# One PSUM tile for two banks, merged adds among the last pairs, and pair 4 loaded in blocks, in a matmul with rotary embedding

## The chip, the core and the metric

The kernel runs on one core of a Trainium2 chip. The metric is the device time of one execution in microseconds. A run executes the kernel under test and the kernel before in turn on the same chip. A ratio is the mean time of one kernel's fast executions over the mean of the other's in the same rounds, so it is not quite the ratio of the medians quoted beside it, which take in all executions. A profile shows one execution, the profiled one.

## The reference

The input is 16 x 512 rows of 768 numbers. All are multiplied by one 768 x 768 matrix, and each 64-wide head of the product is rotated (a "rope").

```python
y = np.matmul(x, weight)                      # x: (16, 512, 768)
y = y.reshape(batch, seq, n_heads, head_dim)  # 12 heads of 64
y1, y2 = y[..., :32], y[..., 32:]
out1 = y1 * cos1 - y2 * sin1                  # cos, sin: (512, 64)
out2 = y2 * cos2 + y1 * sin2
out = np.concatenate([out1, out2], axis=-1)
```

## The kernel before

The 64 units of work have 128 rows each; two units make a pair, so there are 32 pairs (0 to 31). I call the halves of pair 3 "3a" and "3b". A unit is loaded, cast to 16 bits, transposed, multiplied (12 matmuls in the plain case), multiplied by cosine and sine on VectorE (the rope, which reads PSUM) and added up on GpSimd; then the pair is stored.

There are three ways to load and transpose. A **plain pair** comes as two full loads of 384 KB, is cast on ScalarE, transposed on TensorE and copied from PSUM by ScalarE. A **block pair** of the first kind comes as four quarter loads of 192 KB from the SyncE queue; each writes 32 of the 128 partitions in runs of 768 bytes. ScalarE casts it, VectorE transposes it, and TensorE is spared two groups of six transposes. A block pair of the second kind is loaded and cast by GpSimd's DMA queue.

```python
BLOCKS = range(8, 25, 4)              # second kind: 8, 12, ... 24
BLOCKS_SP = (*range(6, 27, 4), 28)    # first kind: 6, 10, ... 26, 28
...
hpool = ...tile_pool(name="hpool", bufs=2)              # block pairs of the first kind
py_pool = ...tile_pool(name="py", bufs=6, space=PSUM)   # six single banks
...
def load_quarter(n, q, eng, dst):     # q-th block of columns -> partitions 32q to 32q+31
    src = x[b : b + 2].rearrange("b (j a r) (q k) -> r q a (b j) k", r=SB, a=R, q=NQ)
    dst = dst.rearrange("p s (j k) -> p (s j) k", j=NQ)
    eng.dma_start(out=dst[ts(q, R)], in_=src[r, q])
...
def psum(n, s):                       # a pair has three banks; each of the last four has 2 x 2
    key, banks = (n, 3) if n < NP - ALONE else ((n, s), 2)
...
for n in range(2, AHEAD - 1):         # pairs 2 to 5, two full loads each
    load_pair(n)
for q in (0, 2, 1, 3):                # then pair 6 in quarters
    load_blocks_sp(AHEAD - 1, q)
...
for n in range(2, NP):
    load_pair(n + AHEAD - 2)
    for q, ahead in ((0, 8), (2, 7), (1, 6), (3, 5)):
        if n + ahead >= AHEAD:
            load_blocks_sp(n + ahead, q)
    ...
    for s in (0, 1):
        i = 2 * n + s
        if n < 4:
            for c0, c1 in ((0, 256), (256, H)):
                for c in CHUNKS:
                    mm(n, s, *c, c0, c1)
                if c0 == 0:
                    upto("turn", i + 2)   # transposes and ScalarE's copies of what is ahead
                    upto("cast", i + 4)   # ScalarE's casts of what is still further ahead
        ...
```

In the views, PE is TensorE, PEld its weight loads, DVE VectorE, ACT ScalarE, POOL GpSimd and SP SyncE; a q marks the issue of an instruction or a transfer. The tile xs holds a plain unit, xf a block pair of the first kind, xh one of the second, xc the cast, xT the transposed unit, psy (and later psw) the product in PSUM, pt a transpose in PSUM, tq the rope, ov the sum.

On ScalarE instructions go in the order of the program (its lines in the views stand in that order: before, the cast of 4a at 21.93 us, then the copy of 3b at 23.52 us). In the loop above, while unit 5 (2b) is multiplied, the cast of unit 8 (4a) is put on ScalarE; the copy of unit 7 (3b) is put there one unit later, so behind that cast. ScalarE also issues the stores of most pairs.

## Time and profile before

| | before |
|---|---|
| median of three executions | 156.14 us |
| span of the profiled execution | 152.3 us |
| TensorE busy | 145.4 us (95%) |
| VectorE, GpSimd busy | 131.2 us, 123.6 us |
| granted TensorE clock | 0.994 |

The span is the time from the first to the last instruction. The decisive view is the chain of work that ended last: TensorE has 92% of it, without a gap. The lines stand in the prediction. The view by windows: after the window (us) come busy times of TensorE, its weight loads, VectorE, ScalarE and GpSimd, then the granted clock, the busy share of the DMA engines and GB/s.

```profile
16.00:22.00 6.00, 6.00 (x56) 4.55 (x55) 6.00 (x6) 4.68 (x7) 4.45 (x6) 1.00 1.04 374
```

### The profile page before, as it was taken

The page shows a single profiled execution, that of the slowest core. Times are in us where ns is not written, and L with a number is a line of the kernel's source. Part 1 is how long each engine was busy: PE and PEld are TensorE (multiplying, and loading weights), DVE is VectorE, ACT ScalarE, POOL GpSimd, SP SyncE. Part 2 cuts the span into 40 slices and gives each one's busy share as a digit, 9 for nine tenths or more (in the row PEclk, how much of TensorE's full clock was granted, in tenths as well). Part 3 has the DMA queues.
Part 4 walks back from the last instruction along what each step waited for, and adds up shares of the span by engine and source line. Part 5 has one row for each costly group of instructions (what it writes and reads, how often), then busy time and mean ns, then how long its engine had stood idle before and what let it go on. Part 6 is the DMA issues. An engine that isn't in the chain of part 4 may idle for free.

```text
span 152.3 us, 2721 instructions
## 1 busy us (share of the span) xinstructions
PE 145.4 (95%) x1038; PEld 92.2 (61%) x1038; DVE 131.2 (86%) x140; ACT 73.6 (48%) x91; POOL 123.6 (81%) x72
## 2 busy tenths in 40 slices
PE   6999999999999999999999999999999999999950
PEld 2556777666656566666656665666666566666620
DVE  0567999779898989989898989989898989997890
ACT  3260696882525726282616624582617547764200
POOL 1000399999998999799997999787888879999990
PEclk9999999999999999999999999999999999999997
DMA  5999999999999999999999999999999999996555
GB/s 134 377 401 400 404 320 244 271 387 340 300 302 405 375 304 356 355 397 291 363 330 347 400 341 239 358 400 402 320 330 404 414 410 401 409 373 235 203 205 195
DMA packets 29037, 51.17 MB, mean 336 GB/s; under 512 B 7264, under 2 KB 15072, under 8 KB 29024
## 3 DMA queue, kind: packets, MB, share of 16 engines
q1 hardware_dynamic: 16640, 29.17, 56.9%
q10 hardware_dynamic: 6944, 19.86, 33.1%
q0 software_dynamic: 5440, 1.97, 10.7%
q8 instruction: 8, 0.13, 0.4%
q14 instruction: 5, 0.04, 0.1%
HBM read 27.79 MB, written 25.17 MB: 348 GB/s over the span
## 4 chain that ended last, share of the span: by engine, by line
PE 92%; DVE 5%; issue 0%; DVEq 0%
PE psy L174 79%; PE pt L140 9%; PE psy L254 4%; DVE tq L188 3%; DVE psy L225 0%; DVE ov L229 0%; DVE xT L78 0%; DVE cold L261 0%; DVE w_sb L126 0%; DVEq L229 0%; DVE tq L225 0%; DVEq L188 0%
## 5 line engine op out<-in xcount | busy, mean ns | idle before, releaser
L174 PE MATMUL psy<-w_sb,xT 128*128 128x256 f16 (+2 forms) x781 | 131.1, 323 | 0.2 <-DVE w_sb L126 0.2
L188 DVE TENSOR_TENSOR tq<-psy,csn 128x1024 f32<-128x1024 f32 (+1 forms) x99 | 111.6, 1167 | 9.6 <-PE psy L174 9.3
L199 POOL TENSOR_TENSOR ov<-tq 128x1536 f32<-128x1536 f32 (+2 forms) x45 | 111.3, 2501 | 8.1 <-DVE tq L188 5.4
L174 PEld LDWEIGHTS <-xT 128*128 128x128 f16 x781 | 74.7, 98 | 44.8 <-ACT xc L76 0.5
L76 ACT COPY xT<-pt 128x768 f16<-128x768 f16 x38 | 30.4, 799 | 57.8 <-PE pt L140 53.5
L76 ACT CAST xc<-xs 128x768 f16<-128x768 f32 x38 | 33.1, 909 | 9.7 <-DMA xs<-in_x_dram 7.7
L140 PEld LDWEIGHTS <-xc 128*128 128x128 f16 x240 | 17.1, 100 | 5.8 <-DVE xc L78 0.9
L140 PE MATMUL pt<-ident,xc 128*128 128x128 f16 x240 | 20.4, 222 | 0.0
L331 POOL COPY mark<-xs 128x1 f32<-128x1 f32 x1 | 0.2, 185 | 15.8 <-DMA xs<-in_x_dram 15.8
L76 ACT CAST xc<-xf 128x768 f16<-128x768 f32 x14 | 12.7, 906 | 0.0
L99 POOL DMA_DIRECT2D xh<-in_x_dram x20 | 11.8, 595 | 0.5 <-issue 0.5
L254 PE MATMUL psy<-cold 128*128 128x512 f16 x17 | 6.9, 557 | 1.2 <-DVE cold L261 1.2
L148 DVE STREAM_TRANSPOSE xT<-xc 128x384 f32<-128x384 f32 x14 | 7.9, 563 | 0.0
L148 DVE STREAM_TRANSPOSE xT<-xh 128x384 f32<-128x384 f32 x10 | 7.0, 700 | 0.0
L126 DVE CAST w_sb<-w_raw 128x768 f16<-128x768 f32 (+2 forms) x7 | 3.4, 500 | 1.7 <-DMA w_raw<-in_weight_dram 1.7
L78 DVE CAST xc<-xs 128x768 f16<-128x768 f32 x2 | 1.9, 948 | 3.2 <-DMA xs<-in_x_dram 3.2
L254 PEld LDWEIGHTS <-cold 128*128 128x128 f16 x17 | 2.0, 131 | 3.5 <-issue 2.2
L78 DVE COPY xT<-pt 128x768 f16<-128x768 f16 x2 | 1.1, 558 | 1.6 <-PE pt L140 1.6
L76 ACT ACT_TABLE_LOAD x1 | 1.3, 1283 | 0.7 <-PEq L408 0.7
L261 DVE MEMSET cold<- 128x256 uint32 x1 | 0.3, 272 | 0.9 <-PEq L408 0.9
L229 DVE TENSOR_TENSOR ov<-psy,tq 128x384 f32<-128x384 f32 x1 | 0.6, 558 | 0.0
L225 DVE TENSOR_TENSOR tq<-psy,csn 128x384 f32<-128x384 f32 x1 | 0.6, 557 | 0.0
(9 smaller groups left out, 1.9 us busy)
## 6 DMA issues: line engine op xcount, KB each, us to landing
out_dram<-ov ACTq DMA_DIRECT2D x25, 768.0 KB, 8.8
xs<-in_x_dram SPq DMA_DIRECT2D x40, 384.0 KB, 9.0
xf<-in_x_dram SPq DMA_DIRECT2D x28, 192.0 KB, 10.3
out_dram<-ov SPq DMA_DIRECT2D x7, 384.0 KB, 2.4
out_dram<-ov SPq DMA_DIRECT2D x3, 768.0 KB, 7.0
w_raw<-in_weight_dram SPq DMA_DIRECT2D x5, 384.0 KB, 6.7
xh<-in_x_dram POOLq DMA_DIRECT2D x20, 96.0 KB, 10.1
w_raw<-in_weight_dram SPq DMA_DIRECT2D x1, 256.0 KB, 5.4
```

The costliest lines, as they stand in the source:

```text
L76: eng.copy(out=o, in_=i_)
L78: eng.tensor_copy(out=o, in_=i_)
L99: eng.dma_start(out=dst[ts(q, R)], in_=src[r, q])
L126: nc.vector.tensor_copy(out=w_sb[:, t, e, c0:c1], in_=w_raw[t, e][:, c0:c1])
L140: nc.tensor.transpose(pt[:, t, e, :], xc[:, t, e, :], ident)
L148: nc.vector.transpose(out=xT.bitcast(FP32).rearrange("p t (j a) o -> p t j (a o)", j=NQ), in_=x16.pop((n, s)).bitcast(FP32).rearrange(orde ...
L174: nc.tensor.matmul(ps[:, a - lo : z - lo], xTT[n, s][:, t, e, :], w_sb[:, t, e, a:z], start=((t, e) == CHUNKS[0] and n > 1), stop=((t, e) ...
L188: nc.vector.tensor_tensor(out=tqs[n][:, :, c0:c1].rearrange("p j (h d) -> p j h d", d=D), in0=ps.rearrange("p (h d) -> p h d", d=D) .unsqu ...
L199: eng.tensor_tensor(out=ovs[n][:, ds(c0, w)].rearrange("p (h t d) -> p h t d", t=2, d=HD), in0=tq[:, 0].rearrange("p (h t d) -> p h t d", ...
L225: nc.vector.tensor_tensor(out=o, in0=ph, op=MULT, in1=csn[:, j, n % SB, :].unsqueeze(1).broadcast_to((P, nh, D)),)
L229: nc.vector.tensor_tensor(out=ovs[n][:, c0:c1].rearrange("p (h t d) -> p h t d", t=2, d=HD), in0=ps.rearrange("p (h t d) -> p h t d", t=2, ...
L254: nc.tensor.matmul(psys[n][b], cold[:, 0:P], cold, start=True, stop=opened[0] < WARM - 6)
```

## The change

It has three intents: two of a pair's three PSUM banks become one wide tile, so that one rope of 2048 elements does the work of two of 1024; the first halves of pairs 28 to 30 get one rope, and all their halves one add; pair 4 becomes a block pair of the first kind, which takes two groups of transposes from TensorE. The third part also changes the order of the first loads, the distances at which quarters are fetched ahead, and the number of buffers for block pairs.

```diff
-    BLOCKS_SP = (*range(6, 27, 4), 28)
+    BLOCKS_SP = (4, *range(6, 27, 4), 28)
...
-    hpool = ctx.enter_context(tc.tile_pool(name="hpool", bufs=2))
+    hpool = ctx.enter_context(tc.tile_pool(name="hpool", bufs=3))
...
-    py_pool = ...(name="py", bufs=6, space=bass.MemoryType.PSUM)
+    py_pool = ...(name="py", bufs=2, space=bass.MemoryType.PSUM)   # 2 single, 2 double
...
+    def bank(wide):
+        return py_pool.tile([P, 1024 if wide else 512], FP32, tag="psw" if wide else "psy", ...)
...
     def rope_bank(n, b):
-        rope(n, b * 512, (b + 1) * 512, psys[n][b])
+        rope(n, 512 * b, 512 * (1 + 2 * b), psys[n][b])
...
-    for n in range(2, AHEAD - 1):
-        load_pair(n)
-    for q in (0, 2, 1, 3):
-        load_blocks_sp(AHEAD - 1, q)
+    load_pair(2)
+    load(3, 0)
+    load_blocks_sp(4, 0)
+    load(3, 1)
+    load_blocks_sp(4, 2)
+    load(5, 0)
+    load_blocks_sp(4, 1)
+    load(5, 1)
+    for m, q in ((4, 3), (6, 0), (6, 2), (6, 1), (6, 3)):
+        load_blocks_sp(m, q)
...
-        for q, ahead in ((0, 8), (2, 7), (1, 6), (3, 5)):
+        for q, ahead in ((0, 7), (2, 6), (1, 6), (3, 5)):
...
+            if not in_halves(n, s):                  # 28a, 29a, 30a
+                for c in CHUNKS:
+                    mm(n, s, *c)
+                rope(n, s * H, (s + 1) * H, psys[n, s][:, 0:H])
+                add(n, s * H, (s + 1) * H, nc.gpsimd)
+                store(n, nc.sync, s * H, (s + 1) * H)
+                continue
...
-                add(n, c0, c1, nc.gpsimd)
+                if n == NP - 1:
+                    add(n, c0, c1, nc.gpsimd)
+                elif hi == H:
+                    add(n, s * H, (s + 1) * H, nc.gpsimd)
```

More of the change, by code (lines that the diff above doesn't have):

```diff
@@ L69 @@
     pt_pool = ctx.enter_context(tc.tile_pool(name="pt", bufs=2, space=bass.MemoryType.PSUM))
-    py_pool = ctx.enter_context(tc.tile_pool(name="py", bufs=6, space=bass.MemoryType.PSUM))
+    py_pool = ctx.enter_context(tc.tile_pool(name="py", bufs=2, space=bass.MemoryType.PSUM))
     w_raw, xss, xhs, x16, xTT, psys, tqs, ovs = {}, {}, {}, {}, {}, {}, {}, {}
@@ L152, in transpose_blocks, with in_halves @@
         xTT[n, s] = xT.rearrange("p t m e -> p t e m")
-    def psum(n, s):
-        key, banks = (n, 3) if n < NP - ALONE else ((n, s), 2)
-        if key not in psys:
-            psys[key] = [
-                py_pool.tile([P, 512], FP32, tag="psy", name="psy") for _ in range(banks)
-            ]
-        ps = psys[key]
-        if banks == 2:
-            return [(ps[k][:, 0:HH], k * HH, (k + 1) * HH) for k in (0, 1)]
-        cut = 512 if s == 0 else 256
-        return [(ps[s][:, ds(s * 256, cut)], 0, cut), (ps[s + 1][:, 0 : H - cut], cut, H)]
+    def bank(wide):
+        return py_pool.tile(
+            [P, 1024 if wide else 512], FP32,
+            tag="psw" if wide else "psy", name="psw" if wide else "psy",
+        )
+    def in_halves(n, s):
+        return s == 1 or n == NP - 1
+    def psum(n, s):
+        if n < NP - ALONE:
+            if n not in psys:
+                psys[n] = bank(False), bank(True)
+            one, two = psys[n]
+            if s == 0:
+                return [(one, 0, 512), (two[:, 0:256], 512, H)]
+            return [(two[:, 256:512], 0, 256), (two[:, 512:1024], 256, H)]
+        if not in_halves(n, s):
+            if (n, s) not in psys:
+                psys[n, s] = bank(True)
+            ps = psys[n, s]
+            return [(ps[:, 0:512], 0, 512), (ps[:, 512:H], 512, H)]
+        if (n, s) not in psys:
+            psys[n, s] = [bank((n, s) == (NP - 1, 1)) for _ in (0, 1)]
+        ps = psys[n, s]
+        return [(ps[k][:, 0:HH], k * HH, (k + 1) * HH) for k in (0, 1)]
     def mm(n, s, t, e, c0=0, c1=H):
@@ L213, in rope_pair @@
     def rope_pair(n):
-        for b in range(3):
+        for b in (0, 1):
             rope_bank(n, b)
@@ L253, in warm @@
             psum(n, 0)
+            ps = psys[n][0] if b == 0 else psys[n][1][:, ts(b - 1, 512)]
             nc.tensor.matmul(
-                psys[n][b], cold[:, 0:P], cold, start=True, stop=opened[0] < WARM - 6
+                ps, cold[:, 0:P], cold, start=True, stop=opened[0] < WARM - 6
             )
@@ L368 @@
             if n < NP - ALONE:
-                for b in ((0,), (1, 2))[s]:
-                    rope_bank(n, b)
+                rope_bank(n, s)
+                continue
+            if not in_halves(n, s):
+                for c in CHUNKS:
[3 more added lines that the diff above has]
+                store(n, nc.sync, s * H, (s + 1) * H)
                 continue
```

## The prediction

> **What bounds the kernel now.** I read the shares of busy time first, then the chain of waits that ended last, then the timelines of the stretches that the diff touches: the first 32 us, where pair 4 is loaded, and the last 25 us, where the last pairs end.
>
> ```profile
> PE 145.4 (95%) x1038; PEld 92.2 (61%) x1038; DVE 131.2 (86%) x140; ACT 73.6 (48%) x91; POOL 123.6 (81%) x72
> ...
> PE 92%; DVE 5%; issue 0%; DVEq 0%
> PE psy L174 79%; PE pt L140 9%; PE psy L254 4%; DVE tq L188 3%; DVE psy L225 0%; DVE ov L229 0%; DVE xT L78 0%; DVE cold L261 0%; DVE w_sb L126 0%; DVEq L229 0%; DVE tq L225 0%; DVEq L188 0%
> ```
>
> TensorE carries 92% of the chain, VectorE only the end. The same chain in order of time shows TensorE without a gap:
>
> ```profile
> 23.15 0.33 PE pt L140 x6
> 23.48 1.97 PE psy L174 x18
> 25.45 0.33 PE pt L140 x6
> 25.79 1.29 PE psy L174 x6
> 27.08 0.34 PE pt L140 x6
> 27.41 1.95 PE psy L174 x12
> ```
>
> One unit (half a pair, 12 matmuls) is 1.95 us, a group of six transposes 0.33 to 0.34 us. So only TensorE's own work, or a new hole in it, moves the time much. VectorE waits 7.9 us for TensorE between 20 and 126 us, and GpSimd 5.4 us for VectorE between 60 and 126 us: both keep up there. At the end all three finish together: TensorE's last matmul at 146.8 us, then three short VectorE operations:
>
> ```profile
> 146.84 0.56 DVE L225 TENSOR_TENSOR tq<-psy,csn 128x384 f32<-128x384 f32 x1
> 147.32 0.56 DVE L225 TENSOR_TENSOR psy<-psy,csn 128x384 f32<-128x384 f32 x1
> 147.91 0.56 DVE L229 TENSOR_TENSOR ov<-psy,tq 128x384 f32<-128x384 f32 x1
> ```
>
> which end at 148.47 us. GpSimd's last adds (130.46 us plus 18.00 us, no gap) end at 148.46 us.
>
> [...] 1024-element ropes go in chains of one in 1.18, two in 2.35, three in 3.45 us; each costs about its elements. [...] ScalarE's casts and copies stand in the order of the program. A cast that waits for data therefore holds the copies behind it. [...]
>
> **The change part by part.** *Pair 4 as a block pair.* Its two groups of TensorE transposes go (2 x 0.335 = 0.67 us off the path) and with them two ScalarE copies of 0.80 us. VectorE gets two stream transposes of 0.56 us, which it can hide. Price: its two loads of 384 KB become four quarter loads of 192 KB in runs of 768 B, and a cast of either half needs all four quarters. Now the order of landing counts. Each load's landing is its issue plus its time to landing: before, pair 3's halves land at 17.0 and 18.0 us, pair 4's at 19.0 and 19.9, pair 5's at 22.7 and 24.4 (13.8 + 8.9, 14.2 + 10.2), pair 6's last quarter at 30.1 (18.0 + 12.1). The step grows from 0.97 us because GpSimd's own small loads then share the engines; the bandwidth falls:
>
> ```profile
> 18.00:20.00 2.00, 2.00 (x24) 1.83 (x22) 2.00 (x3) 1.06 (x2) 2.00 (x4) 1.00 1.06 406
> 20.00:22.00 2.00, 2.00 (x19) 1.45 (x18) 2.00 (x3) 2.00 (x4) 1.99 (x2) 1.00 1.04 317
> 22.00:24.00 2.00, 2.00 (x22) 1.62 (x20) 2.00 (x3) 1.33 (x3) 2.00 (x2) 1.00 1.26 220
> ```
>
> (last columns: granted clock, DMA share, GB/s). In the new order (3a, 4q0, 3b, 4q2, 5a, 4q1, 5b, 4q3, then pair 6) pair 4's last quarter stands behind both loads of pair 5. How long is a quarter? At 400 GB/s 0.49 us; from the stretch 110 to 112 us, where quarters run nearly alone at 231 GB/s, 0.85 us; I choose 0.65 us, as here they alternate with full loads. From 17.0 us: 4q0 17.65, 3b 18.6, 4q2 19.3, 5a 20.2, 4q1 20.9; then contention: 5b 2.2 us, 4q3 1.2 us, so about 24.3 us.
>
> When is it needed? ScalarE's order is cast of 4a, copy of the transposed 3b, cast of 4b:
>
> ```profile
> 21.93 0.92 ACT L76 CAST xc<-xs 128x768 f16<-128x768 f32 x1
> 23.52 0.80 ACT L76 COPY xT<-pt 128x768 f16<-128x768 f16 x1 [0.67 <-PE pt L140]
> ```
>
> The copy of 3b feeds TensorE's matmuls at 24.78 us (23.48 plus 12 matmuls of 0.108). It must start by 23.95, so the cast must start by about 23.1 us (0.82 us from a cast to what follows). With landing at 24.3 us TensorE stands 1.2 us. After it pair 4's transposes on VectorE come in time (cast of 4b would end near 26.7 us, unit 9 starts near 30), and pair 6, later by four quarters less two loads (4 x 0.65 - 1.94 = 0.7 us), finds TensorE later by as much. Net of this part: -0.67 + 1.2 = +0.5 us.
>
> *Second and third bank as one tile.* 28 pairs have two ropes of 1024 elements become one of 2048. From the means 1205 and 953 ns for 1024 and 768 elements the slope is 0.98 ns, so one of 2048 is about 2.21 us against 2.35 for two: 0.14 us each, under 4 us of VectorE in all, beside TensorE: nothing on the path. Both banks now come free together, but pair n + 2 needs them some 4 us after; the rope ends about 2.3 us after its unit, so no wait. TensorE's work is unchanged.
>
> *The last four pairs.* First halves of pairs 28 to 30 get one rope of 1536 elements (estimate 0.953 + 768 x 0.00098 = 1.71 us, against 1.86 for two), all six halves one add instead of two: 6 x (2 x 0.96 - 1.80) = 0.7 us less GpSimd. But the small tiles are only two now: 30's second half takes both and 31's first half follows at once. Call P the end of 30's first half on TensorE. The rope runs from P to P + 1.71; 30b's first quarter-tile can be roped only from about P + 1.63 to P + 2.58, while TensorE wants that bank at P + 0.34 + 1.95 = P + 2.29. It waits about 0.34 us with the signal. Before, with six banks in turn, there is no such wait. GpSimd, followed through the same way, ends its last add near P + 8.16, VectorE near P + 8.23, against P + 7.85 before. So +0.4 us; the saved adds are used up by their later start, as one add waits for both ropes.
>
> Sum: -0.67 + 1.2 + 0.34, that is +0.87 us, on 156.14: **157.0 us**.
>
> **The rivals.** *The quarters arrive in time.* For it: whoever wrote this interleaved the loads with care, and if a quarter costs 0.5 us among full loads the last lands near 23 us and there is no hole. Then -0.67 + 0.34 = -0.3: 155.8 us. Against it: four of them need to overlap, with 220 GB/s at the time. I give it a quarter. *The hole is larger.* At 0.95 us a quarter (the time of the queue's packets, 56.9% of the span, less its other bytes at the stores' rate, shared among 28 quarters) the last lands past 25.5 us, a hole of 2.4 to 4 us: 158.3 to 159.8 us. [...] *VectorE becomes the bound* through two more transposes: it had 7.9 us of waiting, and merging gives more than 1.1 us back, so no. *GpSimd ends last before, and fewer adds help at once*: it ends 0.01 us before VectorE, so at best they save nothing alone.
>
> **Range and chances.** From the first rival with a little noise, 155.5, to a hole of 2.8 us, 158.6. Faster by over 2% needs under 153.0, and nothing on the path offers 3 us: 0.01. Slower by over 2% needs over 159.3, a hole of 3.5 us: 0.06. The rest, 0.93, is within 2%.
>
> **What would show it.** In the changed trace: TensorE transposes 228 instead of 240; ScalarE's cast of pair 4 preceded by a wait for the load near 24 us, then a hole in TensorE's chain near 25 us of 0.5 to 2.5 us, and none if the first rival holds; a wait of about 0.3 us of TensorE for VectorE just before 31's first half; 28 ropes of 1024 elements and 28 of 2048 in place of 84 of 1024, VectorE's busy time down by some 3 us, without effect; last add and last VectorE operation again within 0.2 us. Wrong would make it: quarters that land before 23 us, a stall later in the middle because a prefetch moved, or small banks freed earlier than I work out.

## The result and the profile after

The changed kernel took 164.78 us (median of four, 162.18 to 165.3) against 155.83 us for the kernel before in the same rounds. The ratio of the fast executions is 1.0481, with a 95% interval of 1.0328 to 1.0634. It is slower by nearly 5%, and outside the predicted range. Two of the four executions lie over 1.5% above the fastest and do not count as fast; that leaves two, hence the wide interval.

These are lines of the page of the changed kernel: busy times, then TensorE's busy tenths and granted clock in 40 slices of 4.07 us, then the chain that ended last by engine.

```profile
PE 148.0 (91%) x1026; PEld 91.8 (56%) x1026; DVE 130.4 (80%) x111; ACT 72.0 (44%) x89; POOL 122.7 (75%) x66
...
PE   7999993399999999999999999999899899999870
...
PEclk9999999659999999999999999999999999999999
...
PE 53%; DMA 23%; DVE 11%; POOL 4%; issue 3%; SPq 2%; ACT 1%; ACTq 1%; DVEq 0%
```

Three things are to be seen. TensorE has 12 instructions less (1026 for 1038), as intended, yet more busy time. In the seventh and eighth slice it is three tenths busy, and in the eighth and ninth its clock is at six and five tenths. And transfers, which had no part in the chain before, now have 23% of it. The same chain in order of time shows where it leaves TensorE:

```profile
16.64 12.78 DMA xf<-in_x_dram
...
29.76 0.41 ACTq L260
...
30.31 0.81 ACT xT L76
...
31.16 4.02 PE psw L190 x12
```

The transfer is the last quarter of pair 4. It was issued at 16.64 us and landed 12.8 us later. ScalarE's own order of time shows who waited for it:

```profile
22.51 0.79 ACT L76 COPY xT<-pt 128x768 f16<-128x768 f16 x1
29.52 0.88 ACT L76 CAST xc<-xf 128x768 f16<-128x768 f32 x1 [6.23 <-DMA xf<-in_x_dram]
29.76 0.41 ACTq L260 DMA_DIRECT2D out_dram<-ov  x1
30.31 0.80 ACT L76 COPY xT<-pt 128x768 f16<-128x768 f16 x1
```

ScalarE stood idle for 6.23 us ahead of the cast of 4a; the copy behind that cast is that of 3b, which TensorE needed next. TensorE stood 5.33 us. What follows the hole is in the windows:

```profile
16.00:22.00 6.00, 5.94 (x56) 4.45 (x55) 6.00 (x5) 3.99 (x6) 3.07 (x6) 1.00 1.09 224
...
26.00:30.00 4.00, 0.00 (x0) 0.00 (x0) 1.05 (x1) 0.47 (x1) 4.00 (x2) 0.96 1.33 220
30.00:36.00 6.00, 4.84 (x15) 2.24 (x16) 1.94 (x3) 3.43 (x5) 1.79 (x1) 0.50 1.10 294
```

From 16 to 22 us only 224 GB/s arrive, for 374 before, with the DMA engines no less busy (share 1.09 for 1.04). From 30 to 36 us the clock is 0.50: the two units from 31.16 to 37.84 us took 6.68 us, where two units take 3.90 us at the full clock.

The accounts of the two profiled executions, by when TensorE reaches the same work: the transposes of 5a start at 29.37 us before and at 37.84 us after, 8.47 us later. The hole and a small one ahead of it (0.29 us) make 5.6 us, the low clock 2.8 us, a later start of this execution 0.57 us, and the two transpose groups give back 0.67 us; that sums to 8.3 us. The last transposes start at 140.46 and 150.59 us, 10.13 us later, so the middle loses another 1.7 us. The last VectorE operation ends at 148.47 and 159.25 us, 10.78 us later, so the tail loses some 0.65 us.

### The profile page after: what moved, and what is told of

Read it like the earlier page. It is cut to its first block, busy times and chain, and to the rows that moved or that the text cites.

```text
span 162.8 us, 2672 instructions
## 1 busy us (share of the span) xinstructions
PE 148.0 (91%) x1026; PEld 91.8 (56%) x1026; DVE 130.4 (80%) x111; ACT 72.0 (44%) x89; POOL 122.7 (75%) x66
## 4 chain that ended last, share of the span: by engine, by line
PE 53%; DMA 23%; DVE 11%; POOL 4%; issue 3%; SPq 2%; ACT 1%; ACTq 1%; DVEq 0%
PE psw L190 33%; PE psy L190 16%; DVE tq L204 9%; DMA xf<-in_x_dram 8%; DMA out_dram<-ov 7%; POOL ov L215 4%; DMA xs<-in_x_dram 4%; DMA w_raw<-in_weight_dram 4%; PE pt L140 4%; DVE xT L148 1%; SPq L83 1%; ACT xT L76 1%; SPq L123 1%; ACTq L260 0%; ACT xc L76 0%
## 5 line engine op out<-in xcount | busy, mean ns | idle before, releaser
L190 PE MATMUL psw<-w_sb,xT 128*128 128x256 f16 (+2 forms) x552 | 113.1, 314 | 5.3 <-ACT xT L76 5.3
L204 DVE TENSOR_TENSOR tq<-psw,csn 128x2048 f32<-128x2048 f32 (+2 forms) x32 | 69.9, 2186 | 14.8 <-PE psw L190 12.4
L190 PE MATMUL psy<-w_sb,xT 128*128 128x512 f16 (+2 forms) x229 | 66.2, 359 | 2.1 <-ACT xT L76 1.1
L76 ACT COPY xT<-pt 128x768 f16<-128x768 f16 x36 | 28.7, 798 | 58.5 <-PE pt L140 47.1
L204 DVE TENSOR_TENSOR tq<-psy,csn 128x1024 f32<-128x1024 f32 (+1 forms) x36 | 41.0, 1147 | 1.7 <-PE psy L190 1.6
L76 ACT CAST xc<-xs 128x768 f16<-128x768 f32 x36 | 31.1, 901 | 14.5 <-DMA xs<-in_x_dram 10.3
L140 PE MATMUL pt<-ident,xc 128*128 128x128 f16 x228 | 19.1, 220 | 1.0 <-ACT xc L76 0.7
L76 ACT CAST xc<-xf 128x768 f16<-128x768 f32 x16 | 14.5, 903 | 6.2 <-DMA xf<-in_x_dram 6.2
L271 PE MATMUL psw<-cold 128*128 128x512 f16 x11 | 4.9, 518 | 0.0
L271 PE MATMUL psy<-cold 128*128 128x512 f16 x6 | 3.3, 545 | 1.2 <-DVE cold L278 1.2
```

Source lines behind the costliest of these rows:

```text
L76: eng.copy(out=o, in_=i_)
L140: nc.tensor.transpose(pt[:, t, e, :], xc[:, t, e, :], ident)
L190: nc.tensor.matmul(ps[:, a - lo : z - lo], xTT[n, s][:, t, e, :], w_sb[:, t, e, a:z], start=((t, e) == CHUNKS[0] and n > 1), stop=((t, e) ...
L204: nc.vector.tensor_tensor(out=tqs[n][:, :, c0:c1].rearrange("p j (h d) -> p j h d", d=D), in0=ps.rearrange("p (h d) -> p h d", d=D) .unsqu ...
L271: nc.tensor.matmul(ps, cold[:, 0:P], cold, start=True, stop=opened[0] < WARM - 6)
```

## The experiments

My theory was that the late quarters of pair 4, seen through ScalarE's strict order, make the hole, and that the hole makes the low clock. The first rival was the wide PSUM tile: its two banks come free together and later. Later rivals are told where they arise. All twelve kernels gave right results.

| run | what it is | median us | ratio to before, 95% interval |
|---|---|---|---|
| changed kernel | | 164.78 | 1.0481 (1.0328 to 1.0634) |
| e1 | pair 4 part undone | 155.04 | 1.0000 (0.9976 to 1.0023) |
| e2 | pair 4 part alone | 162.88 | 1.0530 (1.0467 to 1.0594) |
| e3 | pair 4's quarters in a row | 157.06 | 1.0131 (1.0104 to 1.0158) |
| e4 | copy of 3b ahead of the cast of 4a | 159.48 | 1.0261 (1.0200 to 1.0322) |
| e5 | hole filled with matmuls of zeros | 160.16 | 1.0327 (1.0280 to 1.0373) |
| e6 | quarters spread over 128 partitions | 159.29 | 1.0263 (1.0197 to 1.0329) |
| e7 | e3, and GpSimd's loads later | 157.92 | 1.0138 (1.0080 to 1.0196) |
| e8 | e1, wide tile roped in halves | 159.28 | 1.0277 (1.0230 to 1.0324) |
| e9 | quarters two by two | 157.16 | 1.0111 (1.0034 to 1.0189) |
| e10 | e1, spare banks for 31a | 155.09 | 1.0004 (0.9976 to 1.0031) |
| e11 | e1, new prefetch distances and buffer | 158.56 | 1.0226 (1.0161 to 1.0290) |
| e12 | e3, old prefetch distances | 158.80 | 1.0209 (1.0134 to 1.0285) |

### e1 and e2: which part

e1 is the changed kernel with `BLOCKS_SP`, `hpool`, the first loads and the prefetch distances as before. e2 is the kernel before with exactly these four changed.

> The changed kernel with pair 4 loaded and transposed as before (load order, prefetch distances and buffer count as before); the merged PSUM tile and the new tail stay. Theory 1 (the late quarters of pair 4 make the hole): no hole of TensorE near 25 us, no low clock, 155.5 to 157 us. What the tail costs (about +0.4 us by my prediction) shows here alone. Rival (the merged PSUM tile or its later release makes the loss): still 160 us or more.

> The kernel before with only the pair 4 part of the change (block pair, its load order, three buffers). Theory 1: the hole of some 5 us near 25 us and the low clock after it, 162 to 165 us. Rival (merged tile): 155 to 156.5 us. If both parts are needed together, in between.

e1 is as fast as the kernel before, and e2 as slow as the changed kernel. The rival is out: the wide tile and the tail cost nothing that the times resolve, and the pair 4 part alone makes the loss. In e2's profile the cast of 4a waits again for its last quarter (landed at 28.0 us):

```profile
28.11 0.89 ACT L76 CAST xc<-xf 128x768 f16<-128x768 f32 x1 [4.81 <-DMA xf<-in_x_dram]
```

### e4: the order on ScalarE

```diff
-                        upto("cast", i + 4)
+                        upto("cast", i + 3 if i == 5 else i + 4)
```

> The changed kernel with one change of order on ScalarE: the cast of pair 4's first half stands after the copy of the transposed second half of pair 3 instead of before it. The loads stay late. Theory 1 (ScalarE's strict order turns the late load into a hole one unit early): TensorE goes on with pair 3's second half (1.95 us), the hole shrinks from 5.3 to some 3.3 us and, if the clock then stays up, the time falls by 2 to 5 us to 159.5 to 162.5 us; the last quarter still lands near 29.4 us. If the order on ScalarE does not matter: 164 us.

It took 159.48 us, at the lower edge of what was expected. By the ratios that is 2.2% less than the changed kernel (1.0261 for 1.0481) and 2.7% less than e2 (1.0530), which has the same pair 4 part and a narrower interval. The last quarter landed at 28.7 us, much as late, but the copy of 3b no longer waited:

```profile
24.34 0.80 ACT L76 COPY xT<-pt 128x768 f16<-128x768 f16 x1 [1.26 <-PE pt L140]
28.81 0.88 ACT L76 CAST xc<-xf 128x768 f16<-128x768 f32 x1 [3.67 <-DMA xf<-in_x_dram]
```

TensorE's hole came one unit later and was 2.8 us long, and the clock stayed at 1.00 after it. So the place of one cast on an in-order engine, with the low clock that its hole brought, accounts for about half of the loss.

### e5: the clock after the hole

26 matmuls of zeros were put ahead of 3b's matmuls, into a bank that these overwrite.

```diff
+                    if (n, s, c0) == (3, 1, 0):
+                        psum(n, s)
+                        for _ in range(26):
+                            nc.tensor.matmul(psys[n][1][:, 512:1024], cold[:, 0:P], cold,
+                                             start=True, stop=True)
```

> The changed kernel with 26 matmuls of zeros (128x512, 0.216 us each, 5.6 us in all) put on TensorE at the place of the hole; they write a bank that the next matmuls overwrite, so the result is right. The hole itself stays. If the clock drop after the hole is a cost of its own (in the profile of the changed kernel 12 + 12 matmuls took 6.68 us from 31.16 us on, instead of 3.90), the granted clock stays at 1.00 and the time falls by some 2.8 us, to about 161 to 162.5 us. If not, 164 us or more.

It took 160.16 us, somewhat better than expected. By the ratios that is 2.0% less than e2 (1.0327 for 1.0530), clear of the noise; against the changed kernel itself (1.0481) it is 1.5% less, and these two intervals overlap. The clock held:

```profile
30.00:36.00 6.00, 6.00 (x42) 3.75 (x41) 4.00 (x3) 2.99 (x5) 2.14 (x2) 1.00 1.05 355
```

The profile shows the clock's part by itself: the same two units, 3b and 4a, took 3.90 us here (30.26 to 34.16 us) and 6.68 us in the changed kernel, so 2.8 us. Not all of the gain is the clock: in this execution the last quarter landed at 27.7 us, 1.8 us earlier than in the changed kernel's profile (the zeros held TensorE until 30.26 us, which gave half of that away), and TensorE had no wait of 0.2 us or more in the middle.

### e3, e9 and e6: why the quarters are late

e3 puts pair 4's quarters in a row after 3b, e9 two after 3a and two after 3b. e6 keeps the changed kernel's order but sends pair 4's four pieces, with the same source bytes in the same runs of 768 bytes, to all 128 partitions; pair 4 then goes through TensorE again.

```diff
 # e3
+    load_pair(2); load_pair(3)
+    for q in (0, 2, 1, 3): load_blocks_sp(4, q)
+    load_pair(5); ...
 # e9
+    load_pair(2); load(3, 0); load_blocks_sp(4, 0); load_blocks_sp(4, 2)
+    load(3, 1); load_blocks_sp(4, 1); load_blocks_sp(4, 3); load_pair(5); ...
 # e6, in load_blocks_sp, for n == 4
+            nc.sync.dma_start(out=xhs[n][:, :, ts(q, H // NQ)],
+                in_=x[b : b + 2].rearrange("b (p r) h -> r p b h", r=SB)[r, :, :, ts(q, H // NQ)])
```

> The changed kernel with another load order only: both halves of pair 3, then the four quarters of pair 4 in a row, then pair 5. Theory 1a (quarters are slow because they alternate with full loads): a quarter takes 0.85 to 1 us in a row, the last one lands near 22.5 us, hole under 0.5 us, 155.5 to 157.5 us. Theory 1b (a quarter costs near 2 us of the queue wherever it stands, four of them 6 to 8 us): the last one lands at 24.5 to 26.5 us, hole of 1.5 to 3.5 us, 158 to 161 us. Rival (merged tile): 164 us as before.

> The changed kernel with its load order, but pair 4's four pieces land in all 128 partitions (same source bytes, same runs of 768 B, same places in the queue) and pair 4 is transposed on TensorE again. Tells why alternating quarters are slow. If it is the 32 partitions that each quarter writes to: the bandwidth from 16 to 20 us stays near 400 GB/s, a piece plus a full load take some 1.5 us, the last piece lands near 23 to 24 us and the hole is under 1 us: 155.5 to 158 us. If it is the short runs: bandwidth near 200 to 250 GB/s again, last piece near 28 us or later, hole of 4 us or more, 161 us or more.

> The changed kernel with the load order: first half of pair 3, two quarters of pair 4, second half of pair 3, the other two quarters, then pair 5. Theory (while a quarter is in the queue, everything in it, full loads too, goes at the quarters' rate of 190 to 230 GB/s): bandwidth from 17 to 22 us stays near 200 to 240 GB/s, pair 3's second half lands near 20.5 to 21.5 us though only 0.59 MB stand between the first half of pair 3 and its end, the last quarter near 23 us, between the row (21.8) and the alternating order (29.4); 157 to 159.5 us. If it is the number of changes between the kinds, the second half of pair 3 lands by 20 us and the last quarter by 22 us, and the time is that of the row, 157 us.

When the loads landed (us; each is the issue plus the time to landing that the trace shows):

| | before | changed | e3 row | e9 two by two | e6 spread |
|---|---|---|---|---|---|
| 3a | 17.0 | 18.4 | 17.0 | 17.8 | 18.0 |
| 3b | 18.0 | 21.6 | 18.4 | 21.0 | 19.6 |
| pair 4, first quarter | | 19.7 | 19.3 | 18.9 | 18.5 |
| pair 4, complete | 20.0 | 29.4 | 21.8 | 22.8 | 24.9 |
| pair 5, complete | 24.5 | 28.2 | 26.8 | 27.2 | 24.2 |
| pair 6, complete | 30.1 | 34.3 | 31.9 | 32.5 | 30.5 |

The windows of the three, in this order:

```profile
16.00:22.00 6.00, 6.00 (x56) 4.50 (x55) 6.00 (x4) 4.67 (x7) 4.42 (x6) 1.00 1.10 282
```

```profile
16.00:22.00 6.00, 6.00 (x56) 4.51 (x55) 6.00 (x5) 4.42 (x7) 3.65 (x6) 1.00 1.09 253
```

```profile
16.00:22.00 6.00, 5.99 (x58) 4.62 (x56) 6.00 (x4) 4.65 (x6) 3.49 (x6) 1.00 1.06 363
```

In a row a quarter takes 0.8 to 0.9 us (landings at 19.3, 20.2, 21.0, 21.8). Alternating, 4q0 and 3b together take 3.2 us (18.4 to 21.6): more than a quarter in a row (0.85) and a full load alone (0.97) together. Where quarters stand between full loads the full loads slow down too, and everything goes at some 224 GB/s. e9 shows the same in between: 3b landed at 21.0 us, as expected. e6 shows the reason. The same runs of 768 bytes, spread over 128 partitions, arrive at 363 GB/s, for 224 in the changed kernel, a piece in about 0.5 us. So it is not the short runs; it is the 32 partitions.

The last quarter's 29.4 us, against 21.8 us in the row, has two parts. In e3 the same eight loads (pairs 3, 4 and 5) were all in by 26.8 us, so alternating cost 2.7 us (some 0.6 us of it the later start of that execution). The other 4.9 us is the order: in the changed kernel both loads of pair 5 stand ahead of the last quarter, and in e3 behind it.

A quarter in a row goes at 231 GB/s (192 KB, that is 196,608 bytes, in 0.85 us), the whole mixed stretch at 224 GB/s. The row is no clean test of what 32 partitions take, as its quarters go to different partitions in turn (0 to 31, 64 to 95, 32 to 63, 96 to 127). That a full load between quarters slows down with them, the runs show (3.2 us for 4q0 and 3b, for 0.85 and 0.97 us apart), and not why.

e6 was slower in sum than I expected. Its early hole is 1.0 us, near what was expected, but two more waits of TensorE, 2.2 and 1.1 us, came past 80 us. e3 ended within its first case, but at its upper end: no early wait above 0.5 us, but others of 1.6 us in sum past 80 us. That called for the next runs.

### e7, e11 and e12: the waits in the middle

e7 is e3 with GpSimd's first four loads (for pair 8) after its first two adds. e11 is e1 with the changed prefetch distances and the third buffer, e12 is e3 with the old distances.

```diff
 # e7
-    nc.gpsimd.tensor_copy(out=mark, in_=xss[3, 0][:, 0:1]); load_blocks(...); load_blocks(...)
     ...
     rope_pair(1)
+    nc.gpsimd.tensor_copy(out=mark, in_=xss[3, 0][:, 0:1]); load_blocks(...); load_blocks(...)
 # e11, against e1
-    hpool ... bufs=2          ((0, 8), (2, 7), (1, 6), (3, 5))
+    hpool ... bufs=3          ((0, 7), (2, 6), (1, 6), (3, 5))
 # e12, against e3
-        for q, ahead in ((0, 7), (2, 6), (1, 6), (3, 5)):
+        for q, ahead in ((0, 8), (2, 7), (1, 6), (3, 5)):
```

> Pair 4's quarters in a row as in the third run, and GpSimd's first four small loads (pair 8) issued after the adds of pairs 0 and 1 instead of before them. If the late pairs 5 and 6 of the third run (holes of about 2 us) are due to these loads sharing the engines, pair 6 lands 3 us earlier, the holes go and the 0.67 us of the two transpose groups shows: 154.3 to 155.5 us. If the short runs alone are too slow, 156.5 to 157.5 us.

> The first run (pair 4 undone) with the changed prefetch distances and the third buffer for block pairs, the last piece of the pair 4 part that no run has alone. In the changed kernel TensorE also stood some 1.5 us in the middle, near 114 and 126 us. If the distances cause it: waits of TensorE for ScalarE between 80 and 127 us, 0.7 us or more in sum, and 155.7 to 157 us. If the block load of pair 4 causes it: no such wait, 155 us, ratio 1.000.

> The third run (pair 4's quarters in a row) with the prefetch distances of the kernel before, third buffer kept. If the distances cost the third run its 2 us: 155 to 156 us, no waits of TensorE in the middle. If the extra time of the queue for pair 4 costs them: 156.5 to 157.5 us, with the waits.

e7 was a miss: 157.92 us, no better than e3. Pair 6 did land earlier (30.2 us), and TensorE had no early wait above 0.3 us, but it waited 2.6 us further on. It shows one thing more. GpSimd's loads were now issued only from 25.5 us on, and still pair 5, between quarters of pairs 4 and 6, took 4.0 us from the last quarter of pair 4 (22.9 to 26.8 us; 4.9 us in e3), where two undisturbed full loads take 1.9 us.

e11 was the surprise. Nothing in it touches pair 4, and it is 2.3% slower. TensorE stood once, for 2.1 us. These are lines of its chain:

```profile
91.39 15.12 DMA xf<-in_x_dram
...
106.59 0.38 ACTq L260
...
107.01 0.89 ACT xc L76
...
107.95 0.51 PE pt L140 x6
```

A quarter load of a later block pair took 15.1 us to land. ScalarE's issue of a store (ACTq, line 260) waited for that landing; behind the store stood the cast that TensorE's next transposes needed. In e1, with the old distances, the same stores go out at 100.3 us and nobody waits. And the clock fell again after the hole:

```profile
108.00:110.00 2.00, 2.00 (x12) 1.10 (x13) 0.00 (x0) 1.40 (x2) 1.81 (x1) 0.62 1.03 269
110.00:112.00 2.00, 2.00 (x9) 0.99 (x8) 0.00 (x0) 0.00 (x0) 0.00 (x0) 0.53 1.11 278
```

In this execution the hole and the clock after it (2.1 us, and 1.7 us worked out from the two windows) make up the 3.9 us by which e11's span exceeds e1's (156.9 and 153.0 us).

Why does a store wait for a load? In all fourteen traces (114 such issues before, 116 in the changed kernel) the loads and stores that SyncE and ScalarE issue use eight semaphores in turn (the packed trace names them, the views do not). No issue starts before the transfer that last had its semaphore has landed, and never more than eight are in flight. So a store's issue waits for whatever transfer stands eight before it in the program. In the changed kernel the last quarter of pair 4 was issued at 16.64 us, right after the landing, at 16.63 us, of the load issued eight before it.

So the new distances and the third buffer together, without pair 4, cost 2.3%. The two were not parted, and the buffer is a live rival. In e1, with two buffers, SyncE stood 4.5 us, until 101.8 us, for a cast to free a buffer before it issued the first quarter of pair 28:

```profile
SPq L99 <- ACT xc L76: 4.5, 1, 4.5
```

The kernel before has the same stop (4.2 us). In e11 there is none: four quarters are issued between 89.9 and 98.9 us, where e1 issues none between 87.6 and 101.8 us. The changed kernel has a store that waits as e11's does, but for another store: one issued at 114.52 us takes 10.9 us to land, ScalarE's store eight transfers later goes out only at 125.46 us, and the copy behind it comes 0.8 us too late for TensorE. With a wait of 0.7 us at 114.8 us, behind a store that waited for GpSimd, that is most of the 1.7 us of the middle.

e12 was a miss, outside both of its cases: with the old distances e3 became no faster (158.8 us; in its profile TensorE waited 2.4 us for ScalarE between 80 and 127 us). So the distances aren't the only cause of such waits once pair 4 comes in quarters. e12 still has the third buffer, so the buffer fits e11 and e12 alike. Whether it is the buffer, the queue's extra time for pair 4 or only another chance meeting of stores and loads stays open; e1 with the third buffer alone would tell.

### e8 and e10: the tail

In e1's profile the wait that the prediction worked out for 31a is there:

```profile
143.61 2.11 PE L190 MATMUL psy<-w_sb,xT 128*128 128x384 f16 x12 [0.48 <-DVE tq L204]
```

e8 ropes the first halves of pairs 28 to 30 in two operations, one from each bank of the wide tile, so that VectorE begins earlier. e10 takes the two banks of the transposes, idle by then, for 31a.

```diff
 # e8, against e1
-            return [(ps[:, 0:512], 0, 512), (ps[:, 512:H], 512, H)]
+            return [(ps[:, 0:HH], 0, HH), (ps[:, 512 : 512 + HH], HH, H)]
 ...
-                for c in CHUNKS:
-                    mm(n, s, *c)
-                rope(n, s * H, (s + 1) * H, psys[n, s][:, 0:H])
+                for ps, lo, hi in psum(n, s):
+                    for c in CHUNKS:
+                        mm(n, s, *c, lo, hi)
+                    rope(n, s * H + lo, s * H + hi, ps)
 # e10, against e1
+            if (n, s) == (NP - 1, 0):
+                psys[n, s] = [pt_pool.tile([P, 512], FP32, tag="pt", name="pt") for _ in (0, 1)]
```

> The kernel with pair 4 undone (first run), and the first halves of pairs 28 to 30 roped again in two operations of 768 elements, each from its own bank of the wide tile; adds stay merged. My account of the tail: the wait of TensorE for VectorE ahead of pair 31 (0.5 us in the profile of the first run) goes and the time falls by 0.3 to 0.5 us against the first run, to about 0.997 of the kernel before. If that wait is no part of the end, the ratio stays at 1.000.

> The kernel with pair 4 undone, and the first half of pair 31 accumulated in the two banks that the transposes no longer use, in place of the two single-bank tiles that pair 30's second half still holds. The only change is which banks. If the 0.5 us wait of TensorE for VectorE ahead of pair 31 is on the path: no such wait, last VectorE operation some 0.3 us earlier, ratio to the kernel before 0.996 to 0.999, 154.5 to 154.9 us. If VectorE or GpSimd is late by itself there, 1.000.

e8 was 159.28 us, and my account of it was wrong in a useful way. The second group of matmuls writes another bank than the one that the first rope reads, but the same tile, and it waited for that rope:

```profile
130.39 1.14 PE L190 MATMUL psw<-w_sb,xT 128*128 128x384 f16 x6
133.48 1.14 PE L190 MATMUL psw<-w_sb,xT 128*128 128x384 f16 x6 [1.95 <-DVE tq L204]
```

Three such waits make 4.2 us. In this kernel a wide tile is waited for as a whole.

e10 did what it should on TensorE (no such wait), and the time stayed: ratio 1.0004. VectorE's last operation started at 148.41 us, but GpSimd's last adds, from 143.05 us on, end at 149.51 us:

```profile
143.05 6.46 POOL L220 TENSOR_TENSOR ov<-tq 128x768 f32<-128x768 f32 x5 [0.16 <-DVE tq L209]
```

One engine's wait was removed and the next one's end stood behind it.

No run beat the kernel before: e1 and e10 equal it within 0.3%.

## Why the prediction was wrong

- **What bounds the kernel**: right. TensorE had no gap before, and the whole loss is made of gaps in it, plus its clock after them.
- **The last quarter of pair 4 would land at about 24.3 us**: wrong, and this is the step that failed. The term was "0.65 us, as here they alternate with full loads". Alternating made it worse, not better: 4q0 and 3b took 3.2 us where I had 1.6. It landed at 29.4 us. Of the 5.1 us that I was short, the four quarters make 1.1 us (4.4 us in sum for 3.25), the full loads among them 2.6 us (3b, 5a and 5b took 6.7 us for 4.05), and 3a, also slowed, 1.4 us (0.6 of it the later start of the execution). So I had priced the narrow pieces and not what they do to their neighbours, which was the larger part. I had the evidence of 231 GB/s for quarters in my own window and read it as a cost to be hidden between full loads; e6 shows that the 32 partitions limit the rate, and e3 that full loads are best kept away from quarters.
- **One more reading behind that step** was wrong as well. I blamed the slow landing of pair 5 on GpSimd's loads; in e7 these come later and pair 5 stays slow (4.0 us, for 4.9 in e3 and 1.9 undisturbed).
- **When it is needed (23.1 us), and that ScalarE's order carries the wait to TensorE**: right. With the landing as measured my own rule gives a hole of 29.4 - 23.1 = 6.3 us, or 5.7 us with the later start of the execution; it was 5.3 us and the small one of 0.3 us ahead. e4 confirms the order.
- **The clock**: the prediction put no cost to it. It cost 2.8 us in the profile; in e5, where it held, the same two units took 2.8 us less. The runs give no length of hole from which on it falls: it was 0.50 after the hole of 5.3 us, 0.62 and 0.53 in the two windows after one of 2.1 us (e11), and still 1.00 after one of 2.8 us (e4), each in one execution.
- **The prefetch distances and the third buffer**: not priced at all. The prediction had them only in its last sentence, as "a stall later in the middle because a prefetch moved". e11 shows that the two together cost 2.3% without pair 4. In the changed kernel the middle lost only 1.7 us, so the costs do not simply add.
- **The wide tile hidden beside TensorE**: right by e1. A rope of 2048 elements took 2.28 us for 2.21 worked out. VectorE's busy time fell by 0.8 us in sum, not 3: a merged rope saves 0.07 us against 2.35 for two, 2.0 us for 28, and the two transposes of pair 4 take back 1.1 us.
- **The tail, +0.4 us**: the wait is there (0.48 us for 0.34), but the ratio of e1 is 1.0000, so no cost of that size is resolved in the time. By e10 the wait and GpSimd's last add end close together.
- **"VectorE becomes the bound"** was rightly dismissed. **"The hole is larger"** was the rival that came true, beyond its own figures; I gave too little weight to it because I took the careful order of the loads for a sign that it had been measured.

## What to carry to other kernels

Before a load is split, look at how many partitions each piece writes; in these runs narrow pieces slowed the full loads that stood between them in the queue (3.2 us for a quarter and a full load that took 0.85 and 0.97 us apart), so keep them together or make them wide. On an in-order engine, put nothing that waits for a late transfer (a cast, or the issue of a store) ahead of what the bounding engine needs next (ScalarE's 6.23 us for the last quarter made TensorE stand 5.33 us), and price the clock after a hole along with the hole (2.8 us here). And part a change that bundles several pieces: here what looked like mere bookkeeping, the prefetch distances with the third buffer, cost 2.3% without the rest. A wait can also come from the count of transfers in flight, eight here.
